# The products of a gated linear recurrence and of its gelu, from GpSimd to VectorE

## The chip, the cores and the metric

One core of a Trainium2 chip runs the whole program in one launch. The metric is the device time of one execution, in microseconds (us); the figure of a kernel is the median of its runs. Engines are named as in the profile: PE (TensorE; PEld its weight loads), DVE (VectorE), ACT (ScalarE), POOL (GpSimd), SP (SyncE, which issues most transfers).

## What is computed

Two transformer blocks over 512 tokens of width 1024, in float32. The change lies in the recurrent branch of the first block alone, 1024 channels wide:

```
gate = gelu(gr)
xc   = conv_b + sum over 4 taps of xpad[:, tap:tap+S] * conv_w[tap]
r    = sigmoid(xblk @ w_a + b_a);   i = sigmoid(xblk @ w_x + b_x)
log_a = -8 * r * softplus(-lru_lambda)
a    = exp(log_a);   b = sqrt(-expm1(2 * log_a)) * (i * xc)
h[t] = a[t] * h[t-1] + b[t]
rnn_out = h * gate
```

`xr` and `gr`, the inputs of the branch, are two of the projections of the first block. The gelu is the tanh form, so its argument is the polynomial `c * (g + 0.044715 g^3)` with `c = sqrt(2/pi)`.

## The kernel before

Activations lie transposed, channels on the 128 partitions and the 512 tokens along the free axis; a "tile" below is one 128x512 block of channels, and the recurrence has eight, tile 0 to tile 7. A float32 product on PE is made of three products of float32r parts: every operand is split into a high part (ACT, L271 `nc.scalar.copy`) and a low part (DVE, L272 `nc.vector.tensor_sub`). Weights arrive as "slabs" of 128x1024: SP loads `raw`, ACT casts `wh`, DVE subtracts `wl` (`slab`, L143), with 3 buffers for `raw` and 4 each for `wh` and `wl`. PE can begin a slab when its `wh` is there, and needs `wl` from the third matmul on.

`lru` (L930) is a generator that runs beside the value projection, the gates of the branch (`gates_T`) and later the first attention heads. `interleave` mixes the streams by a clock of PE's work; the framework's scheduler then fixes each engine's order, which is executed strictly in order. For tile m, `lru` does:

- `conv(m)`: DVE takes the projection `xr` out of PSUM (L937), POOL starts the convolution (L938), DVE adds three taps (L940), and the result `xc` is split into `xsh` and `xsl`.
- `gates(m - 1)`: two products of 3 matmuls each, then on ACT two tanh (L954, L955), a tanh `t2` (L956) and an exp (L957). Between the tables of tanh/exp and of the root ACT loads a table.
- `decay(m - 1)`: three DVE operations (L974 to L976), the root on ACT (L977), then root times d and times `xc` on POOL (L978, L979).
- `gelu(m)`: DVE takes `gr` out of PSUM (L962), ACT squares it (L963), POOL makes the polynomial in two operations (L964, L965), ACT applies tanh (L966).
- `scan(m - 1)`: DVE closes the gelu (L984), multiplies the input gate (L985), runs the scan (L987; ACT prepares its factor at L986), multiplies by the gate (L988), and the result is split into `rnh` (ACT) and `rnl` (DVE).

`rnn_pairs` (L1044) multiplies the eight `rnh`/`rnl` pairs by the next weights. ACT's `rnh` casts stand in one queue with its `wh` casts of the weight slabs.

```
nc.scalar.activation(q, g, AF.Square)
nc.gpsimd.tensor_scalar(q, q, 0.044715 * GELU_C, GELU_C, ALU.mult, ALU.add)
nc.gpsimd.tensor_mul(q, q, g)
```

Of the kernel before, what the change touches and what calls it, by code (L numbers as in the profile page):

```python
# [12 lines left out]
AF = mybir.ActivationFunctionType  # L13
ALU = mybir.AluOpType
# [6 lines left out]
GELU_C = math.sqrt(2.0 / math.pi)  # L21
# [73 lines left out]
class Net:  # L95
# [39 lines left out]
    def col(self, name, i=0, n=1):  # L135
        at, _ = COLS[name]
        return self.cols[:, at + i : at + i + n]
# [792 lines left out]
    def lru(self, act, rnn):  # L930
        nc = self.nc
        cw = lambda m, tap: self.col("conv_w", 4 * m + tap)
        st = {}

        def conv(m, ps):
            xr, xc = self.T("xr"), self.T("xc")
            nc.vector.tensor_mul(xr, ps, self.row)  # L937
            nc.gpsimd.tensor_scalar(xc, xr, cw(m, 3), self.col("conv_b", m), ALU.mult, ALU.add)  # L938
            for d in (1, 2, 3):
                nc.vector.scalar_tensor_tensor(  # L940
                    out=xc[:, d:], in0=xr[:, : S - d], scalar=cw(m, 3 - d), in1=xc[:, d:],
                    op0=ALU.mult, op1=ALU.add,
                )
            st[m] = dict(xc=xc, xs=self.split(xc, None, s="xs"))

        def gates(m):
            e = st[m]
            w = self.slab("w_rg", m, 256)
            pa, px = self.PS(), self.PS()
            self.mm3(pa, (w[0][:, 0:P], w[1][:, 0:P]), e["xs"], True, True)  # L950
            self.mm3(px, (w[0][:, P : 2 * P], w[1][:, P : 2 * P]), e["xs"], True, True)
            tr, ti, t2 = self.T("tr"), self.T("ti"), self.T("t2")
            col = lambda t: t[:, m : m + 1]
            nc.scalar.activation(tr, pa, AF.Tanh, bias=col(self.ba), scale=0.5)  # L954
            nc.scalar.activation(ti, px, AF.Tanh, bias=col(self.bx), scale=0.5)  # L955
            nc.scalar.activation(t2, tr, AF.Tanh, bias=col(self.sp2), scale=col(self.sp2))  # L956
            nc.scalar.activation(tr, tr, AF.Exp, bias=col(self.sp4b), scale=col(self.sp4))  # L957
            e.update(d=tr, ti=ti, t2=t2)

        def gelu(m, ps):  # L960
            g, q = self.T("gr"), self.T("gq")
            nc.vector.tensor_mul(g, ps, self.row)  # L962
            nc.scalar.activation(q, g, AF.Square)  # L963
            nc.gpsimd.tensor_scalar(q, q, 0.044715 * GELU_C, GELU_C, ALU.mult, ALU.add)  # L964
            nc.gpsimd.tensor_mul(q, q, g)  # L965
            nc.scalar.activation(q, q, AF.Tanh)  # L966
            st[m].update(g=g, q=q)

        def decay(m):

            e = st[m]
            d, t2 = e["d"], e["t2"]
            v = self.T("v")
            nc.vector.tensor_scalar_add(d, d, 0.5)  # L974
            nc.vector.scalar_tensor_tensor(out=v, in0=t2, scalar=1.0, in1=d, op0=ALU.add, op1=ALU.mult)
            nc.vector.scalar_tensor_tensor(out=d, in0=v, scalar=-2.0, in1=d, op0=ALU.add, op1=ALU.mult)  # L976
            nc.scalar.activation(t2, t2, AF.Sqrt)  # L977
            nc.gpsimd.tensor_mul(t2, t2, d)  # L978
            nc.gpsimd.tensor_mul(t2, t2, e["xc"])  # L979

        def scan(m):
            e = st.pop(m)
            d, t2, ti, g = e["d"], e["t2"], e["ti"], e["g"]
            nc.vector.scalar_tensor_tensor(out=g, in0=e["q"], scalar=1.0, in1=g, op0=ALU.add, op1=ALU.mult)  # L984
            nc.vector.scalar_tensor_tensor(out=ti, in0=ti, scalar=1.0, in1=t2, op0=ALU.add, op1=ALU.mult)  # L985
            nc.scalar.activation(d, d, AF.Copy, scale=-2.0, bias=-1.0)  # L986
            nc.vector.tensor_tensor_scan(t2, d, ti, 0.0, ALU.mult, ALU.add)  # L987
            nc.vector.scalar_tensor_tensor(out=t2, in0=t2, scalar=-0.5, in1=g, op0=ALU.mult, op1=ALU.mult)  # L988
            rnn.append(self.split(t2, None, s="rn"))

        for m in range(9):
            if m < 8:
                ps = yield from self.proj_T("w_xr", m, act)
                conv(m, ps)
            if m == 8:
                self.lru_tail = True
                yield 0.0
                yield self.lag(0.0, self.o["lg"])
            if m > 0:
                gates(m - 1)  # L1000
                yield 6.0
            if m < 8:
                gen = self.proj_T("w_gr", m, act)
                for _ in range(2):
                    yield next(gen)
                if m > 0:
                    decay(m - 1)
                ps = yield from gen
                gelu(m, ps)
            else:  # L1010
                yield 12.0
                decay(m - 1)
                yield 12.0
            if m > 0:
                scan(m - 1)
# [795 lines left out]
```

## Time and profile before

| what | value |
|---|---|
| median of 3 runs | 1905.67 us (1904.08 to 1912.12) |
| the profiled execution | 1912.68 us |
| its span, first to last instruction | 1910.9 us |
| busy share of the span | PE 98%, DVE 72%, ACT 45%, POOL 13% |
| mean granted TensorE clock | 0.988 of full speed |
| the recurrence, tile 0 to tile 7 | about 65 to 257 us of the span |

Times of day ("at 154.4") are us from the start of the span. A granted clock of 1.00 is 2.4 GHz, 0.50 is 1.2 GHz. In a timeline a row is one instruction or a run of equal ones, with the idle time of the engine just before it, and what ended that, in brackets. Durations of neighbouring rows on one engine overlap slightly.

### The profile page before, as it was taken

How to read it: one execution, taken by the hardware profiler on the slowest of the kernel's cores; microseconds unless marked ns; L12 is line 12 of the kernel's file. 1: busy time of each engine (PE TensorE's matmuls, PEld its weight loads, DVE VectorE, ACT ScalarE, POOL GpSimd, SP SyncE). 2: the span in 40 equal slices, each digit the busy share in tenths (PEclk: the TensorE clock that was granted, in tenths of full speed). 3: DMA queues.
4: the chain of work that ended last, by engine and by line, in shares of the span. 5: the costliest groups of instructions: out<-in, count | busy, mean ns of one | idle time of the engine just before them, and what ended most of it. 6: DMA issues, size and time to landing. Idle time of an engine off the chain costs nothing.

```text
span 1910.9 us, 26868 instructions
## 1 busy us (share of the span) xinstructions
PE 1866.7 (98%) x10392; PEld 1605.4 (84%) x10392; DVE 1366.8 (72%) x2582; ACT 868.5 (45%) x1499; POOL 239.1 (13%) x250
## 2 busy tenths in 40 slices
PE   8999999999989999999999999999999999999997
PEld 7887767888879999998887788888888899989896
DVE  7577787686788787776667856446556799887874
ACT  5456655454354334334334444233434555444443
POOL 3223310200300000002012110132300000000002
PEclk9999999999999999999999999999999999999998
DMA  5222322221453333334322122232432333322221
GB/s 188 79 93 83 105 67 78 89 77 45 142 172 95 99 110 100 95 103 144 98 78 67 67 83 73 99 122 90 153 129 93 122 110 133 110 89 100 100 85 60
DMA packets 57967, 192.23 MB, mean 101 GB/s; under 512 B 7040, under 2 KB 10144, under 8 KB 57840
## 3 DMA queue, kind: packets, MB, share of 16 engines
q1 hardware_dynamic: 50016, 170.78, 27.3%
q0 software_dynamic: 4832, 15.02, 2.6%
q10 hardware_dynamic: 2992, 4.72, 0.7%
q8 instruction: 81, 1.33, 0.3%
q14 instruction: 46, 0.38, 0.1%
HBM read 182.06 MB, written 8.43 MB: 100 GB/s over the span
## 4 chain that ended last, share of the span: by engine, by line
PE 80%; DVE 10%; ACT 4%; DMA 3%; issue 2%; POOL 1%; DVEq 0%; ACTq 0%; POOLq 0%; SPq 0%
PE ps L160 57%; PE u L160 10%; PE v L160 4%; PE p L160 2%; PE s L160 2%; PE o L160 2%; DVE wl L272 2%; PE pv L160 1%; PE pt L164 1%; DMA raw<-in_w_fd 1%; DMA raw<-in_w_fg 1%; ACT wh L271 1%; PE ps L164 1%; DMA raw<-in_w_down 1%; DMA raw<-in_w_fu 0%
## 5 line engine op out<-in xcount | busy, mean ns | idle before, releaser
L160 PE MATMUL ps<-xx,wh 128*128 128x512 f32 x1424 | 448.4, 396 | 2.7 <-ACT wh L271 2.7
L271 ACT CAST wh<-raw 128x1024 fp32r<-128x1024 f32 (+4 forms) x252 | 255.4, 1017 | 340.0 <-PE ps L160 195.6
L272 DVE TENSOR_TENSOR wl<-raw,wh 128x1024 fp32r<-128x1024 f32 (+4 forms) x252 | 313.1, 1243 | 84.1 <-ACT wh L271 82.3
L160 PEld LDWEIGHTS ps<-xx,wh 128*128 128x128 f32 x1424 | 263.8, 189 | 59.5 <-ACT wh L271 3.1
L160 PE MATMUL ps<-xx,wl 128*128 128x512 f32 x712 | 279.7, 393 | 1.6 <-DVE wl L272 1.6
L160 PE MATMUL ps<-wh,xx 128*128 128x512 f32 (+1 forms) x512 | 157.2, 380 | 5.7 <-ACT wh L271 5.7
L160 PEld LDWEIGHTS ps<-xx,wl 128*128 128x128 f32 x712 | 134.6, 189 | 31.7 <-DVE wl L272 2.5
L160 PEld LDWEIGHTS ps<-wh,xx 128*128 128x128 f32 x512 | 95.7, 192 | 22.2 <-ACT wh L271 5.7
L160 PE MATMUL ps<-ul,wh 128*128 128x512 f32 x256 | 100.1, 391 | 0.0
L160 PE MATMUL ps<-uh,wh 128*128 128x512 f32 x256 | 99.9, 391 | 0.0
L160 PE MATMUL ps<-uh,wl 128*128 128x512 f32 x256 | 99.6, 389 | 0.0
L160 PE MATMUL ps<-wl,xx 128*128 128x512 f32 (+1 forms) x256 | 96.7, 378 | 0.0
L480 POOL TENSOR_TENSOR sq<-sq,sq 128x512 f32<-128x512 f32 (+1 forms) x34 | 41.4, 1218 | 310.4 <-ACT sq L477 310.2
L375 ACT CAST sah<-sa 128x1024 fp32r<-128x1024 f32 x38 | 40.0, 1052 | 83.4 <-DVE sa L373 76.0
L160 PE MATMUL ps<-fah,wh 128*128 128x512 f32 (+1 forms) x200 | 73.6, 369 | 1.5 <-ACT fah L274 1.5
L160 PE MATMUL ps<-fal,wh 128*128 128x512 f32 (+1 forms) x200 | 73.4, 367 | 0.1
L160 PE MATMUL ps<-fah,wl 128*128 128x512 f32 (+1 forms) x200 | 72.8, 364 | 0.0
L1079 DVE TENSOR_TENSOR x<-ps,x 128x512 f32<-128x512 f32 x64 | 44.0, 688 | 39.0 <-PE ps L160 38.8
L160 PE MATMUL v<-f2h,wl 128*128 128x256 f32 x304 | 60.9, 283 | 0.0
L160 PEld LDWEIGHTS ps<-uh,wl 128*128 128x128 f32 x256 | 48.1, 188 | 10.3
L160 PEld LDWEIGHTS ps<-wl,xx 128*128 128x128 f32 x256 | 49.2, 192 | 8.3 <-DVE wl L272 0.4
L160 PEld LDWEIGHTS ps<-uh,wh 128*128 128x128 f32 x256 | 48.2, 188 | 9.2 <-ACT uh L271 0.3
(453 smaller groups left out, 4949.9 us busy)
## 6 DMA issues: line engine op xcount, KB each, us to landing
raw<-in_w_up SPq DMA_DIRECT2D x32, 512.0 KB, 3.5
raw<-in_w_down SPq DMA_DIRECT2D x32, 512.0 KB, 3.6
raw<-in_w_gate SPq DMA_DIRECT2D x24, 512.0 KB, 3.4
raw<-in_w_qkv SPq DMA_DIRECT2D x23, 512.0 KB, 3.6
raw<-in_w_fg SPq DMA_DIRECT2D x22, 512.0 KB, 3.4
raw<-in_w_fu SPq DMA_DIRECT2D x22, 512.0 KB, 3.5
raw<-in_w_fd SPq DMA_DIRECT2D x16, 512.0 KB, 3.4
raw<-in_w_conv SPq DMA_DIRECT2D x12, 512.0 KB, 3.5
```

What stands on the lines that cost most here:

```text
L160: self.nc.tensor.matmul(out, **k)
L164: self.nc.tensor.transpose(out, a, ident)
L271: nc.scalar.copy(hi, src)
L272: nc.vector.tensor_sub(lo, src, hi.bitcast(F32))
L375: nc.scalar.copy(ha, sa)
L480: eng.tensor_add(sq[0][:, sl], sq[0][:, sl], sq[1][:, sl])
L1079: nc.vector.tensor_add(self.x[m], ps, self.x[m])
```

## The change

The two products of the root, and the gelu's polynomial, move from POOL to DVE. The polynomial becomes one operation: the square is scaled on ACT in the operation that was there before, and one `scalar_tensor_tensor` adds the constant and multiplies by `g`. POOL keeps L938 alone of the recurrence. Per tile three DVE operations come and four POOL operations go.

```
         def gelu(m, ps):
             g, q = self.T("gr"), self.T("gq")
             nc.vector.tensor_mul(g, ps, self.row)
-            nc.scalar.activation(q, g, AF.Square)
-            nc.gpsimd.tensor_scalar(q, q, 0.044715 * GELU_C, GELU_C, ALU.mult, ALU.add)
-            nc.gpsimd.tensor_mul(q, q, g)
+            nc.scalar.activation(q, g, AF.Square, scale=math.sqrt(0.044715 * GELU_C))
+            nc.vector.scalar_tensor_tensor(out=q, in0=q, scalar=GELU_C, in1=g, op0=ALU.add, op1=ALU.mult)
             nc.scalar.activation(q, q, AF.Tanh)
...
             nc.scalar.activation(t2, t2, AF.Sqrt)
-            nc.gpsimd.tensor_mul(t2, t2, d)
-            nc.gpsimd.tensor_mul(t2, t2, e["xc"])
+            nc.vector.tensor_mul(t2, t2, d)
+            nc.vector.tensor_mul(t2, t2, e["xc"])
```

In the changed kernel one line is gone, so that later lines are numbered one lower: the polynomial is L964, the root L976, its products L977 and L978, the input gate L984, the scan L986, the multiplication by the gate L987. The scheduler also orders other instructions anew, between the second tile and the first pair of attention heads; elsewhere the order of every engine is as before. Numbers in names count buffers, and differ between the kernels.

ACT's queue at the end of tile 2 before, from the root to the split of the scan's result (`rnh`); `wh_1356` is the next slab that PE needs.

```order
L977 ACT_TABLE_LOAD
L977 ACTIVATE t_1171<-t_1171 128x512
L963 ACTIVATE gq_1249<-gr_1248 128x512
L986 ACTIVATE tr_1169<-tr_1169 128x512
L966 ACT_TABLE_LOAD
L966 ACTIVATE gq_1249<-gq_1249 128x512
L271 CAST rnh_1260<-t_1171 128x512
L271 CAST wh_1356<-raw_1355 128x1024
L1023 ACTIVATE gt_1295<-gt_1295 128x512
```

The same place with the change, where that slab is `wh_1352`.

```order
L976 ACT_TABLE_LOAD
L976 ACTIVATE t_1168<-t_1168 128x512
L963 ACTIVATE gq_1246<-gr_1245 128x512
L985 ACTIVATE tr_1166<-tr_1166 128x512
L965 ACT_TABLE_LOAD
L965 ACTIVATE gq_1246<-gq_1246 128x512
L271 CAST wh_1352<-raw_1351 128x1024
L271 CAST rnh_1256<-t_1168 128x512
L271 CAST wh_1399<-raw_1398 128x1024
```

The slab's cast stands ahead of the cast of the scan's result; at tile 1 the same swap is made, at the other tiles not.

DVE's queue at tile 6 before, from the operand d to the end of the scan.

```order
L976 SCALAR_TENSOR_TENSOR tr_1850<-v_1876,tr_1850 128x512
L272 TENSOR_TENSOR wl_2092<-raw_2090,wh_2091 128x1024
L985 SCALAR_TENSOR_TENSOR ti_1851<-ti_1851,t_1852 128x512
L987 SCALAR_TENSOR_TENSOR t_1852<-tr_1850,ti_1851 128x512
L988 SCALAR_TENSOR_TENSOR t_1852<-t_1852,gr_1769 128x512
```

The same with the change.

```order
L975 SCALAR_TENSOR_TENSOR tr_1843<-v_1869,tr_1843 128x512
L272 TENSOR_TENSOR wl_2084<-raw_2082,wh_2083 128x1024
L977 TENSOR_TENSOR t_1845<-t_1845,tr_1843 128x512
L964 SCALAR_TENSOR_TENSOR gq_1889<-gq_1889,gr_1888 128x512
L978 TENSOR_TENSOR t_1845<-t_1845,xc_1660 128x512
L984 SCALAR_TENSOR_TENSOR ti_1844<-ti_1844,t_1845 128x512
L986 SCALAR_TENSOR_TENSOR t_1845<-tr_1843,ti_1844 128x512
L987 SCALAR_TENSOR_TENSOR t_1845<-t_1845,gr_1763 128x512
```

The two products and the polynomial stand between the slab's low part and the input gate. On PE, four more transposes of the first attention heads (L164, `ps<-ident,z`) stand ahead of the first matmul on tile 6's `rnh`: ten in place of six.

## Rows read from the trace of the kernel before

**Rows 1.** Windows by stretch: us, busy (x instructions) of each engine, PEclk, DMA share, GB/s

```profile
64.00:256.00 192.00, 181.23 (x778) 148.06 (x777) 131.00 (x167) 109.17 (x151) 55.51 (x46) 0.96 0.28 87
96.00:128.00 32.00, 32.00 (x143) 26.50 (x142) 22.01 (x30) 19.27 (x30) 11.14 (x9) 1.00 0.31 99
...
130.00:140.00 10.00, 9.15 (x40) 7.22 (x39) 8.50 (x12) 4.87 (x7) 1.67 (x1) 1.00 0.23 71
...
151.50:154.40 2.90, 0.24 (x2) 0.01 (x1) 2.79 (x5) 1.56 (x2) 0.00 (x0) 1.00 0.00 0
154.40:155.90 1.50, 0.72 (x2) 0.28 (x2) 1.50 (x3) 1.15 (x2) 0.00 (x0) 0.76 0.00 0
155.90:161.60 5.70, 5.70 (x13) 4.46 (x14) 4.95 (x6) 2.30 (x4) 1.67 (x1) 0.50 0.38 115
...
242.50:247.20 4.70, 4.70 (x16) 3.91 (x17) 2.49 (x4) 4.02 (x7) 0.87 (x2) 0.50 0.04 11
...
256.30:300.00 43.70, 42.88 (x231) 33.81 (x231) 33.74 (x100) 23.90 (x56) 0.00 (x0) 1.00 0.27 85
```

**Rows 2.** Waits of PE from 60 to 270 us: us in total, times, longest

```profile
PE ps L160 <- ACT rnh L271: 5.5, 1, 5.5
PE ps L160 <- ACT wh L271: 2.7, 1, 2.7
PE ps L160 <- DVE wl L272: 1.6, 2, 0.9
PE ps L160 <- ACT xsh L271: 0.8, 1, 0.8
```

**Rows 3.** Timeline of ACT at the end of tile 2

```profile
144.53 0.63 ACT L977 ACTIVATE t<-t 128x512 f32<-128x512 f32 x1
...
147.48 1.28 ACT L966 ACT_TABLE_LOAD   x1
...
152.77 0.62 ACT L271 CAST rnh<-t 128x512 fp32r<-128x512 f32 x1 [1.97 <-DVE t L988]
153.30 1.04 ACT L271 CAST wh<-raw 128x1024 fp32r<-128x1024 f32 x1
```

**Rows 4.** Timeline of DVE at tile 2

```profile
144.63 0.68 DVE L976 SCALAR_TENSOR_TENSOR tr<-v,tr 128x512 f32<-128x512 f32 x1
...
148.92 1.77 DVE L985 SCALAR_TENSOR_TENSOR ti<-ti,t 128x512 f32<-128x512 f32 x1 [3.27 <-POOL t L979]
150.79 1.23 DVE L987 TENSOR_TENSOR_SCAN t<-tr,ti 128x512 f32<-128x512 f32 x1
152.05 0.69 DVE L988 SCALAR_TENSOR_TENSOR t<-t,gr 128x512 f32<-128x512 f32 x1
```

**Rows 5.** Groups by line and shape, 60 to 260 us: busy us, mean ns, idle before

```profile
L978 POOL TENSOR_TENSOR t<-t,tr 128x512 f32<-128x512 f32 x8 | 11.6, 1452 | 74.5 <-ACT t L977 48.6 <-DVE tr L976 26.0
L979 POOL TENSOR_TENSOR t<-t,xc 128x512 f32<-128x512 f32 x8 | 11.2, 1401 | 0.6
...
L985 DVE SCALAR_TENSOR_TENSOR ti<-ti,t 128x512 f32<-128x512 f32 x8 | 9.8, 1224 | 17.5 <-POOL t L979 17.5
...
L272 DVE TENSOR_TENSOR rnl<-t,rnh 128x512 fp32r<-128x512 f32 x8 | 5.9, 731 | 1.8 <-ACT rnh L271 1.4
...
L975 DVE SCALAR_TENSOR_TENSOR v<-t,tr 128x512 f32<-128x512 f32 x8 | 5.5, 689 | 0.2
L974 DVE TENSOR_SCALAR tr<-tr 128x512 f32<-128x512 f32 x8 | 3.4, 426 | 9.0 <-ACT tr L957 9.0
```

**Rows 6.** Timelines of DVE and PE around tile 6

```profile
221.58 0.68 DVE L937 TENSOR_TENSOR xr<-ps,row 128x512 f32<-128x512 f32 x1
...
233.56 1.22 DVE L272 TENSOR_TENSOR wl<-raw,wh 128x1024 fp32r<-128x1024 f32 x1
...
241.10 0.69 DVE L988 SCALAR_TENSOR_TENSOR t<-t,gr 128x512 f32<-128x512 f32 x1
...
236.21 0.82 PE L164 MATMUL ps<-ident,z 128*128 128x128 f32 x6
```

## The prediction

> **What bounds the kernel now.** I read the windows first, since a share over the whole span says nothing of one stage. PE is the bound: in an undisturbed stretch of the recurrence it never stops, 143 matmuls in 32 us at full clock, so one costs 0.224 us [rows 1]. From 64 to 256 us it was busy 181 of 192 us at a mean clock of 0.96, so this stage has holes; DVE was busy 131 us there and POOL 55.5. Behind the stage, from 256 to 300 us, PE idled 0.8 of 43.7 us: what is won in the stage should arrive at the end.
>
> The waits of PE name the holes [rows 2]: 5.5 us for an `rnh`, 2.7 for a `wh`, 1.6 for a `wl` in two waits, 0.8 for an `xsh`. Two are followed by a second loss. After PE had stood from 151.5 to 154.4 and again between 154.4 and 155.9, it ran until 161.6 at a granted clock of 0.50, which is 1.2 GHz in place of 2.4. After the 5.5 us, from its last transpose before `rnh` at 237.0 [rows 6] to 242.5, it did so for another 4.7 us [rows 1]. The wait of 0.9 us for a `wl` lies between 130 and 140 us, where the clock stayed at 1.00 [rows 1].
>
> So each hole has a price:
>
> - A, end of tile 2. From 151.5 to 161.6, 10.1 us, PE began 15 matmuls (2 and 13) after the last of the work before; they need 15 x 0.224 = 3.4. Lost: 6.7.
> - B, tile 6. 5.5 of standing, and half of the 4.7 us at half clock, 2.3. Lost: 7.8.
> - C and D. The `wl` wait that is not inside A, 0.9, and the `xsh` wait, 0.8. Lost: 1.7.
>
> Together 16.2 us, the most that the change can give, as it touches nothing outside this stage.
>
> **What ends these waits.** A is ended by the cast of a weight slab, but that cast was not slow: ACT stood 1.97 us for L988, cast `rnh`, and only then took the slab [rows 3]. L988 was late because DVE had stood 3.27 us for POOL's second product, and then needed 1.77 us for L985 where POOL was at work [rows 4]; L975, of the same form, takes 0.689 [rows 5]. B is the same chain at tile 6 with `rnh` itself wanted by PE. All eight tiles show DVE waiting for POOL, 17.5 us in all [rows 5].
>
> **The change, part by part.** Removed from the chain: POOL's two products, 1.45 and 1.40 us each tile, with POOL's polynomial between or behind them, and the lengthening of L985, 1224 against 689 ns [rows 5]. Added to DVE: 24 operations of 128x512 with two SBUF operands. The trace of before has no such product of f32 on DVE; the nearest rows are 426 ns (one tensor in) and 731 ns (`rnl`, some of them lengthened by POOL), and L975 at 689 is the same in everything but the arithmetic. I take 0.69: 24 x 0.69 = 16.6 us, in a stage where DVE has 192 - 131 = 61 us idle; its waiting for POOL alone was 17.5. I cost them at nothing as DVE work, and count them in the chain. The scaled square is the ACT operation that was there before. No transfer moves except two loads of bias strips on POOL's queue behind tile 6, which start earlier, and nobody waits for them. The end of the cover would be a DVE without idle time: see the fourth case.
>
> *A, replayed with these durations.* At tile 2 the third step L976 ends at 145.31, the root at 145.16 [rows 3, 4]. On DVE follow in the new order the first product to 146.0, polynomial to 146.7, second product to 147.4, input gate to 148.1, scan (1.23) to 149.3, multiplication by the gate to 150.0, against 152.74 before: 2.7 us earlier. More counts that ACT's slab cast now stands ahead of `rnh`. ACT prepares the scan's factor behind the first product (0.63, to 146.7), loads its table (1.28, to 147.9), applies tanh (0.63 like the root, to 148.6), casts the slab (1.04, to 149.6) [rows 3]. PE wants it at 151.5. `wl` follows on DVE behind the gelu's closing step: 150.0 + 0.69 + 1.22 = 151.9, and PE wants it with its third matmul, 0.45 us behind 151.5. Hole A closes within tenths: I count 6.5 of 6.7. With the products at 0.73 each step is later by 0.04 and nothing changes. C is the same pattern one tile earlier, with the same swap: 0.9.
>
> *B, replayed.* At tile 6 `wl` ends at 234.78 [rows 6]. Then product, polynomial, product, input gate (4 x 0.69) to 237.5, scan to 238.8, L988's counterpart to 239.5, against 241.79: 2.3 us earlier. At tile 5 the chain shortens too, so that DVE takes the last `xr` earlier than at 221.58; it did not wait for PE there [rows 6]. I take 1 us of that, between nothing and 1.5. Four transposes that now stand ahead fill 4 x 0.82 / 6 = 0.5 us. But D goes with the earlier `xr` (0.8), so PE arrives 0.8 sooner. The hole is 5.5 - 2.3 - 1 - 0.5 + 0.8 = 2.5 us. Whether the clock still falls behind it, no row decides: it fell behind the 2.7 us of A, and not behind 0.9. 2.5 is nearer to the former, so I let the 2.3 us at half clock stand. B gives 3.0, and D 0.8.
>
> Since A's end brings PE forward by 6.5 us but the chain by 2.7, the chain must gain the rest on tiles 3 to 5, or be late at tile 6. It should: it sheds 1 to 2 us on each, by the same count. That is the weakest link, and the second case prices it.
>
> *Sum.* 6.5 + 0.9 + 3.0 + 0.8 = 11.2 us. What is late next is tile 7's `rnh`, which PE met without a wait before, and the first attention heads, whose DVE order was made anew. I take 0 for both, between 1 us won and 3 lost, from the 0.8 us that PE idled behind the stage and the 2.5 of a hole like B's remainder.
>
> The profiled execution took 1912.68 us and would take 1901.5. It lies 7.0 above the median of 1905.67, and the three runs spread over 8; against the median the forecast is **1894.5 us**.
>
> **The rivals.**
>
> 1. *As worked out*: A gone, B reduced. 1894.5, between 1889.5 (the whole 16.2) and 1896.
> 2. *B stays whole.* A goes, 6.5, with C; but tiles 3 to 5 do not make up for PE's lead, so the `xr` and the root of tile 6 come no sooner against PE and 0 to 2 of B and D is won. For it: DVE did not wait for PE at the last `xr` [rows 6], so the chain ran by itself there. Against: it sheds POOL's 2.85 us each tile for 1.4. Gain 6.5 + 0.9 + 1 = 8.4 less up to 3 in the heads: 1897 to 1900.
> 3. *Nothing to win*: something else ends the waits just behind POOL, as ACT's table loads of 1.28 us or a buffer of the slabs. Then 0 to 3 us, 1903 to 1906. Against: the cast of `rnh` waited for DVE, and the slab's cast stood behind it alone [rows 3]. That the change does not do what it says is excluded by the order: the four operations are off POOL.
> 4. *Slower: DVE becomes what PE waits for.* In DVE's queue the first product stands waiting for the root, and at tile 5 a `wl` of the next slab stands behind both. If DVE's 131 us and 16.6 more, with new waits, fill the stage, PE waits for `wl` on each tile. It decides when these waits reach 192 - 147.6 = 44 us. Up to 16.6 us, 1922; half of it, 1914, as the lengthened rows come back. Against: at tile 2 the root was done before L976, so the first product waits for nothing. The Trainium skill, in "Perfetto Trace Analysis", section "Optimizing Scalar/DVE Operations", says that work may be worth moving off VectorE, even to GpSimd, where VectorE is saturated; that speaks against the change on this branch alone, and by it the time would be this case's. The trace does not bear the condition out, with VectorE at 131 of 192 us, and the same section doubts that moving work between these two helps at all.
>
> **How the numbers follow.** About 0.5% (9.5 us) is what a measurement of this kernel tells from no change. Case 1: 0.60; its gain of 11.2 lies above that bound by less than the heads could take, which the second case carries. Case 2: 0.26. Case 3: 0.07. Case 4: 0.07. Case 1 counts as faster, 2 and 3 as the same but for 0.02 of case 2 that reach past the bound: 0.62 faster, 0.31 the same, 0.07 slower. The range takes case 1 down to the whole 16.2 and a us or two of the runs' own spread, 1888, and up through case 2 into case 3, 1903. What is left out is case 4 and the end of case 3.
>
> **What would show it.** In the profile after: PE's waits for `wh` at about 150 us and for `wl` at about 133 gone, and full clock from 150 to 160; DVE's 17.5 us of waiting for POOL at the input gate gone, and that operation at 0.69; the products near 0.69 us; PE's wait for tile 6's `rnh` at 2 to 3 us in place of 5.5; POOL's busy time down. Wrong it would be if the products take well over 0.75, if PE waits anew for `wl` or `xsh` in tiles 3 to 6, or if the stage ends 11 us earlier and the heads give it back.

## The result, and the profile after

The changed kernel took 1890.59 us (median of 4 runs, 1887.68 to 1895.34); the kernel before took 1908.29 beside it (4 runs). The ratio is 0.9909, with a 95% interval of 0.9892 to 0.9925: faster by 0.9%, some 17 us, which is more than the 0.5% that a measurement can tell. The profiled execution took 1895.34 us with a span of 1893.6, against 1912.68 and 1910.9.

The first view is PE's waits from 60 to 256 us in the kernel after (columns: us in total, times, longest). It answers to [rows 2].

```profile
PE ps L160 <- ACT rnh L271: 1.6, 1, 1.6
PE ps L160 <- DVE gt L1033: 0.3, 1, 0.3
```

The waits for `wh`, `wl` and `xsh` are gone, and the one for tile 6's `rnh` is 1.6 us in place of 5.5. The windows of the same kernel answer to [rows 1]: length, busy time of PE, PEld, DVE, ACT and POOL, then PE's granted clock, the DMA share and GB/s.

```profile
64.00:256.00 192.00, 190.12 (x865) 155.78 (x864) 151.50 (x237) 120.17 (x175) 13.80 (x14) 1.00 0.32 98
150.00:160.00 10.00, 10.00 (x46) 8.27 (x45) 6.75 (x10) 5.86 (x9) 1.67 (x1) 1.00 0.37 112
224.00:256.00 32.00, 30.12 (x159) 23.30 (x158) 28.26 (x66) 21.39 (x40) 0.00 (x0) 1.00 0.27 81
```

PE was busy 190.12 us of the 192 in place of 181.23, and at full clock throughout. DVE has 151.50 us of work there in place of 131.00, POOL 13.80 in place of 55.51. The groups of instructions from 60 to 250 us (busy us, mean ns of one, idle before and its releaser) answer to [rows 5].

```profile
L977 DVE TENSOR_TENSOR t<-t,tr 128x512 f32<-128x512 f32 x8 | 5.5, 687 | 0.5 <-ACT t L976 0.2
L978 DVE TENSOR_TENSOR t<-t,xc 128x512 f32<-128x512 f32 x8 | 5.5, 687 | 0.1
L964 DVE SCALAR_TENSOR_TENSOR gq<-gq,gr 128x512 f32<-128x512 f32 x8 | 5.5, 686 | 0.5 <-ACT gq L963 0.4
L984 DVE SCALAR_TENSOR_TENSOR ti<-ti,t 128x512 f32<-128x512 f32 x8 | 5.5, 688 | 0.2
L940 DVE SCALAR_TENSOR_TENSOR xc<-xr,cols,xc 128x511 f32<-128x511 f32 x8 | 6.0, 750 | 4.7 <-POOL xc L938 4.7
```

The products and the polynomial take 0.69 us each, DVE's 17.5 us of waiting at the input gate are gone, and that operation (L984, before L985) fell from 1224 to 688 ns. The timelines of DVE and PE at tile 6 answer to [rows 6].

```profile
210.76 0.68 DVE L937 TENSOR_TENSOR xr<-ps,row 128x512 f32<-128x512 f32 x1
...
222.74 1.22 DVE L272 TENSOR_TENSOR wl<-raw,wh 128x1024 fp32r<-128x1024 f32 x1
...
227.85 0.69 DVE L987 SCALAR_TENSOR_TENSOR t<-t,gr 128x512 f32<-128x512 f32 x1
...
226.41 1.25 PE L164 MATMUL ps<-ident,z 128*128 128x128 f32 x10
229.24 0.73 PE L160 MATMUL ps<-rnh,wh 128*128 128x512 f32 x2 [1.58 <-ACT rnh L271]
```

To see whether the gain was kept, I follow the score matmuls of the attention heads (`s`), which come behind the recurrence. This is the tile view of `s` in the kernel before: after the count stand the shortest, median and longest ns, and the start of the first and the last.

```profile
L160 PE MATMUL s<-qkh,qkh x64: 221/398/497, 256.3 to 444.3; 64*128 64x128 f32 x16, 64*128 64x256 f32 x16, 64*128 64x384 f32 x16, 64*128 64x512 f32 x16
```

And in the kernel after:

```profile
L160 PE MATMUL s<-qkh,qkh x64: 221/399/497, 240.4 to 427.6; 64*128 64x128 f32 x16, 64*128 64x256 f32 x16, 64*128 64x384 f32 x16, 64*128 64x512 f32 x16
```

The first `s` starts 15.9 us earlier and the last 16.7; the spans differ by 17.3. All of it was won in the recurrence and the first heads, and kept.

For a single execution a measure is wanted that leaves out what lies around the stage, as the traces begin up to 1.4 us apart, and executions differ behind the stage too. Two matmuls can be told in every trace: the first product of the gates (`xsh`), and the one `s` in the heads that PE begins after a wait for ACT's `zq`. Before and after (PE's timelines):

```profile
83.74 0.39 PE L160 MATMUL ps<-xsh,wh 128*128 128x512 f32 x1
329.27 0.49 PE L160 MATMUL s<-qkh,qkh 64*128 64x512 f32 x1 [0.42 <-ACT zq L762]
...
83.60 0.39 PE L160 MATMUL ps<-xsh,wh 128*128 128x512 f32 x1
312.72 0.49 PE L160 MATMUL s<-qkh,qkh 64*128 64x512 f32 x1 [0.43 <-ACT zq L762]
```

Between the two it is 245.5 us before and 229.1 after. Below, "lead" is by how much this stretch is shorter than the 245.5 of before: 16.4 us for the changed kernel, and 16.4 again in its second profile. The expectations go by the last `s`, which is blurred: from the `s` behind `zq` to the last one it takes 114.9 to 115.1 us in five of the thirteen traces and 113.4 to 113.7 in the others, whatever the kernel. In the five PE ran at half clock for a time between 362 and 392 us, in the others not; it is worth some 1.6 us. These are the windows of two runs that differ by one useless product at tile 6 (told of below, with three and with four products):

```profile
362.00:392.00 30.00, 29.09 (x148) 22.24 (x147) 23.58 (x87) 18.18 (x52) 0.00 (x0) 0.94 0.17 55
...
362.00:392.00 30.00, 29.09 (x159) 22.54 (x158) 25.03 (x89) 19.61 (x55) 0.00 (x0) 1.00 0.19 57
```

### The profile page after: what moved, and what is told of

Read it like the earlier page. It is cut to its first block, busy times and chain, and to the rows that moved or that the text cites. A ratio compares the mean times of both kernels' runs of the same rounds, so it can differ in the third digit from the quotient of the medians.

```text
span 1893.6 us, 26855 instructions
## 1 busy us (share of the span) xinstructions
PE 1859.6 (98%) x10392; PEld 1601.2 (85%) x10392; DVE 1373.4 (73%) x2606; ACT 868.0 (46%) x1499; POOL 197.7 (10%) x218
## 4 chain that ended last, share of the span: by engine, by line
PE 84%; DVE 8%; ACT 3%; issue 2%; DMA 2%; POOL 0%; DVEq 0%; ACTq 0%; POOLq 0%; SPq 0%
PE ps L160 60%; PE u L160 10%; PE v L160 5%; PE p L160 2%; PE s L160 2%; PE o L160 2%; DVE wl L272 1%; PE pv L160 1%; PE pt L164 1%; DMA raw<-in_w_down 1%; ACT L L846 1%; DMA raw<-in_w_fu 0%; PE ps L164 0%; ACT wh L271 0%; DMA raw<-in_w_fg 0%
```

## The experiments

**One half at a time.** The first two kernels make one half of the change. The products alone:

```
-            nc.gpsimd.tensor_mul(t2, t2, d)
-            nc.gpsimd.tensor_mul(t2, t2, e["xc"])
+            nc.vector.tensor_mul(t2, t2, d)
+            nc.vector.tensor_mul(t2, t2, e["xc"])
```

> The two root products on VectorE, the polynomial left on GpSimd as two operations. ACT's order at tiles 1 and 2 is that of the kernel before: the slab's cast stands behind the split of the scan's result. Theory (the chain's length decides): the chain of tile 2 ends 3 us earlier by the products alone, the slab is cast at 151 of the old clock, so hole A is under 1 us without a stretch at half clock, hole B 1 to 2 us; gain 14 to 17 us, nearly the whole. Rival (the new order of ACT's queue decides): A stays at 2 us or more with its half clock; gain 6 to 10 us.

Measured: 1896.81 us, ratio 0.9945 (0.9926 to 0.9964), lead 9.2. The polynomial alone:

```
-            nc.scalar.activation(q, g, AF.Square)
-            nc.gpsimd.tensor_scalar(q, q, 0.044715 * GELU_C, GELU_C, ALU.mult, ALU.add)
-            nc.gpsimd.tensor_mul(q, q, g)
+            nc.scalar.activation(q, g, AF.Square, scale=math.sqrt(0.044715 * GELU_C))
+            nc.vector.scalar_tensor_tensor(out=q, in0=q, scalar=GELU_C, in1=g, op0=ALU.add, op1=ALU.mult)
```

> The polynomial alone on VectorE as one operation, the two root products left on GpSimd. Theory: the chain of each tile loses only the polynomial that stood between the two products (0.7 us) and the lengthening of the input gate (0.5 to 1.1 us), so A shrinks by 1 to 2 us and B by 1 to 2; VectorE still waits over 10 us for GpSimd's second product; gain 2 to 8 us. Rival (GpSimd's shared work as such is the harm, whichever part goes): about half of the 17 us, 8 to 9.

Measured: 1899.58 us, ratio 0.9951 (0.9933 to 0.9969), lead 8.9. Neither expectation came out whole: the products were to win 14 to 17 us with hole B at 1 to 2, and the polynomial was to shrink A by 1 to 2 only. Each half by itself closes hole A: PE keeps a wait of 0.8 us with the products and 0.4 with the polynomial, for a `wl`, and the clock from 150 to 160 us is 1.00 in both. At tile 2 of both kernels ACT still casts `rnh` (at 148.18 and 146.89) ahead of the slab (148.71 and 147.42), so the swap of these two casts was not needed. Hole B stays large in each. PE's timeline, products alone:

```profile
233.22 1.22 PE L160 MATMUL ps<-rnh,wh 128*128 128x512 f32 x2 [3.98 <-ACT rnh L271]
```

And the polynomial alone:

```profile
231.31 1.22 PE L160 MATMUL ps<-rnh,wh 128*128 128x512 f32 x2 [4.64 <-ACT rnh L271]
```

The clock falls behind both: from 224 to 256 us it was 0.89 and 0.95, against 1.00 with the whole change. With the polynomial alone the input gate still waits for POOL's second product on each tile, 12.8 us in all, and the polynomial beside POOL's first product is lengthened from 0.69 to 1.78 us (DVE's timeline at tile 6):

```profile
224.92 1.78 DVE L964 SCALAR_TENSOR_TENSOR gq<-gq,gr 128x512 f32<-128x512 f32 x1
...
227.86 0.69 DVE L984 SCALAR_TENSOR_TENSOR ti<-ti,t 128x512 f32<-128x512 f32 x1 [1.16 <-POOL t L978]
```

With the products alone, the timeline of DVE and POOL at tile 6 shows why:

```profile
226.57 0.93 POOL L964 TENSOR_SCALAR gq<-gq 128x512 f32<-128x512 f32 x1 [11.09 <-ACT gq L963]
226.94 1.10 DVE L978 TENSOR_TENSOR t<-t,tr 128x512 f32<-128x512 f32 x1
227.59 1.60 POOL L965 TENSOR_TENSOR gq<-gq,gr 128x512 f32<-128x512 f32 x1
228.07 1.66 DVE L979 TENSOR_TENSOR t<-t,xc 128x512 f32<-128x512 f32 x1
```

Each product on DVE takes 1.10 and 1.66 us where it takes 0.69 alone, and each ends 0.54 us behind the end of POOL's operation beside it (227.50 and 229.19). The Trainium skill, in "SBUF — State Buffer", section "SBUF: two separate sides", says that a VectorE operation with two inputs in SBUF and a GpSimd operation that reads SBUF exclude one another, and that whichever comes second is blocked until the first is done. The trace agrees: the time behind POOL's end is the same in both rows, whatever the time before it. It is so throughout: in the traces of the kernel before, of the two halves and of the next run, 45 float32 operations of 128x512 on DVE with both operands in SBUF (the scan left aside) began while one of POOL's products or operations of the polynomial ran, and every one ended 0.54 or 0.55 us behind it. The eight that read one operand from PSUM and began beside such an operation took 0.68 or 0.69 us all the same. POOL is held up in its turn: in the traces before and after, its first step of the convolution (L938) took 0.77 us alone, and 1.60 to 1.84 us where DVE had begun the low part of a 128x1024 slab before it, or at most 0.11 us behind it; that low part took its usual 1.22.

**POOL's hindrance by itself.** The changed kernel, with four products on POOL at each tile that feed nothing:

```
             nc.vector.scalar_tensor_tensor(out=v, in0=t2, scalar=1.0, in1=d, op0=ALU.add, op1=ALU.mult)
             nc.vector.scalar_tensor_tensor(out=d, in0=v, scalar=-2.0, in1=d, op0=ALU.add, op1=ALU.mult)
             nc.scalar.activation(t2, t2, AF.Sqrt)
+            for _ in range(4):
+                nc.gpsimd.tensor_mul(self.T("junk"), v, v)
```

> The changed kernel with four products of v by itself on GpSimd in each tile, written to tiles that nobody reads, so that GpSimd works beside the new VectorE chain as it did before, and nobody waits for it. Theory (the hand-over and GpSimd's own slowness were the harm): 0 to 4 us slower than the changed kernel. Rival (GpSimd and VectorE hinder each other, and that was most of it): the VectorE operations beside it lengthen from 0.69 to 1.2 us and more, the wait for tile 6's result grows to 3 us or more with a stretch at half clock, 5 us and more slower than the changed kernel.

Measured: 1911.61 us, ratio 1.002 (1.0002 to 1.0038); the lead is -4.8, 21.2 us less than after the change (the last `s` at 447.2, 19.6 later). The whole gain is gone. The groups from 60 to 250 us:

```profile
L978 POOL TENSOR_TENSOR junk<-v 128x512 f32<-128x512 f32 x28 | 42.5, 1545 | 60.3 <-DVE v L974 60.3
L980 DVE TENSOR_TENSOR t<-t,xc 128x512 f32<-128x512 f32 x7 | 9.7, 1390 | 0.1
L964 DVE SCALAR_TENSOR_TENSOR gq<-gq,gr 128x512 f32<-128x512 f32 x8 | 9.7, 1210 | 0.4 <-ACT gq L963 0.4
L979 DVE TENSOR_TENSOR t<-t,tr 128x512 f32<-128x512 f32 x7 | 7.7, 1098 | 0.2 <-ACT t L976 0.2
```

Nobody waits for these products: DVE's only wait for POOL is the 4.7 us for `xc` that it has after the change too. But they lengthen the three moved operations from 0.69 to 1.39, 1.21 and 1.10 us: 7 x 0.70 + 8 x 0.52 + 7 x 0.41 = 12.0 us. The third step, the input gate and the low parts of the slabs lose another 6 us in the same way (0.69 to 0.93 and 0.85, 1.22 to 1.31, 0.42 to 0.52). The theory that only the hand-over and POOL's slowness were the harm falls.

**VectorE's idle time.** As many useless products on DVE, which test the fourth case of the rivals:

```
             rnn.append(self.split(t2, None, s="rn"))
+            for _ in range(4):
+                nc.vector.tensor_mul(self.T("junk"), t2, t2)
```

> The changed kernel, with four products of 128x512 into tiles that nobody reads on VectorE behind each tile's scan and split, 32 x 0.69 = 22 us in all; VectorE would be busy 173 of the stage's 192 us. They need no other engine. It tests the fourth case of the rivals and stands beside the run with 42.5 us of products on GpSimd. Theory (VectorE's time is spare only off the chain; these stand ahead of the next tile's xr and put it off by 2.8 us, and tiles catch up in part): PE waits again for rnh, xsh or wl, 5 to 15 us in the stage. Case 4 as the prediction counted it (it decides only when waits fill 44 us): nothing or up to 2 us. Rival (VectorE fills at once): 16 us and more, the slower side of the kernel before.

Measured: 1907.94 us, ratio 1.0009 (0.9994 to 1.0025); the lead is -1.0, 17.4 us less than after the change (the last `s` at 442.7, 15.1 later). PE's waits from 60 to 256 us, then the group of the added products from 60 to 250:

```profile
PE ps L160 <- ACT xsh L271: 6.3, 1, 6.3
PE ps L160 <- ACT rnh L271: 4.2, 1, 4.2
PE ps L160 <- DVE wl L272: 0.9, 1, 0.9
...
L990 DVE TENSOR_TENSOR junk<-t 128x512 f32<-128x512 f32 x28 | 17.4, 684 | 0.0
```

DVE had 40 us idle in the stage after the change; with 28 of the added operations in it DVE was busy 156 of the 192 us, and none of its other operations took longer. The chain of the tiles was late all the same. Case 4 as counted (up to 2 us) falls. The loss lies above what I expected (5 to 15) and is as large as the rival had it (16 and more), but not for the rival's reason: VectorE was not full.

**The part of `rnh`.** The kernel before, with the high part made on DVE, so that ACT's queue does not hold a slab's cast behind it:

```
-            rnn.append(self.split(t2, None, s="rn"))
+            hi, lo = self.R("rnh"), self.R("rnl")
+            nc.vector.tensor_copy(hi, t2)
+            nc.vector.tensor_sub(lo, t2, hi.bitcast(F32))
+            rnn.append((hi, lo))
```

> The kernel before, with the high part of the scan's result made on VectorE and no longer on ACT, so that ACT's slab cast waits for no scan. Theory A (PE waits at tile 2 because of ACT's queue alone): hole A closes with its half clock, 5 to 7 us faster than before. Theory B (the slab's low part stands behind the same chain in VectorE's queue, so the chain's length must shrink): PE's wait for the high part turns into one of 3 us for the low part; within 2 us of the kernel before.

Measured: 1909.87 us, ratio 1.0008 (0.9988 to 1.0028), lead -1.1. PE's waits from 60 to 256 us:

```profile
PE ps L160 <- DVE rnh L990: 4.2, 1, 4.2
PE ps L160 <- DVE wl L272: 4.1, 2, 3.7
PE ps L160 <- ACT xsh L271: 2.2, 1, 2.2
```

The wait for `wh` became one of 3.7 us for the `wl` of the same slab, which stands behind the same chain on DVE. Moving the cast alone wins nothing; the chain has to be shorter.

**The size of hole B, and the clock.** In the changed kernel, tile 6's chain alone is made longer by two, three, four and seven products on DVE. The edit, with N for that number:

```
             nc.vector.tensor_mul(t2, t2, e["xc"])
+            if m == 6:
+                for _ in range(N):
+                    nc.vector.tensor_mul(self.T("junk"), v, v)
```

> The changed kernel, with two products of v by v into a tile that nobody reads on VectorE at tile 6 alone, between the root's third step and its scan: the chain of hole B is 2 x 0.69 = 1.4 us longer, at no other place. In the changed kernel PE waits 1.6 us there and the clock stays at 1.00. In the new order four more transposes of 0.125 us stand ahead of PE's wait. Theory (a hole of this size costs itself and no clock, as after the change): the wait is 1.6 + 1.4 - 0.5 = 2.5 us, the clock stays at 1.00 and the stage ends 1 us later. Rival (the prediction's own step, by which the clock falls behind a hole of 2.5 us as it did behind the 2.7 of hole A): the wait is about 2.5, and behind it 3 to 5 us run at half clock, the stage ends 3 to 4 us later. Second rival (the wait is not set by this chain): it stays at 1.6 or below.

> As the run with two products more at tile 6, with three: VectorE's order and PE's are the same but for the one product. There PE stood 1.88 us for rnh and the clock stayed at 1.00. Each product costs 0.60 us start to start, so the wait should be 2.5 us, which is the very hole that the prediction left standing with its half clock. The prediction's step: behind it 3 to 5 us at half clock, and the last score matmul 3 us later than with two. Rival: the clock stays at 1.00, and the stage ends 0.6 us later.

> The same with four products: a wait of 3.1 us. The prediction's step: half clock behind it for 3 to 5 us. Rival (the clock falls with this hole, not with the one before): 1.00 at three products and below it here. Second rival: 1.00 in both.

> The same with seven products, a wait of 4.9 us, close to the 5.5 of hole B before the change. All theories: the clock falls to half for 4 to 5 us behind it; it says that the place does not matter for the clock, and gives the price of such a hole in the new order: the last score matmul 3.0 us later for the standing and 2 more for the clock than with two products, 432.8 us in place of 427.8. If the clock stays at 1.00 here too, it was something else than the hole that lowered it before the change.

PE's wait and the window of 230 to 240 us with two products:

```profile
230.03 0.73 PE L160 MATMUL ps<-rnh,wh 128*128 128x512 f32 x2 [1.88 <-ACT rnh L271]
...
230.00:240.00 10.00, 9.96 (x42) 7.91 (x43) 7.90 (x13) 7.21 (x11) 0.00 (x0) 1.00 0.01 2
```

And with three:

```profile
230.28 0.79 PE L160 MATMUL ps<-rnh,wh 128*128 128x512 f32 x2 [2.48 <-ACT rnh L271]
...
230.00:240.00 10.00, 9.72 (x35) 7.58 (x36) 7.91 (x13) 7.46 (x12) 0.00 (x0) 0.83 0.01 2
232.00:234.00 2.00, 2.00 (x6) 1.57 (x5) 1.25 (x3) 2.00 (x5) 0.00 (x0) 0.50 0.00 0
```

| products added at tile 6 | PE's wait for `rnh` | clock, 230 to 240 us | lead | last `s` |
|---|---|---|---|---|
| none | 1.58 | 1.00 | 16.4 | 427.6 |
| two | 1.88 | 1.00 | 14.5 | 427.8 |
| three | 2.48 | 0.83 | 12.5 | 431.1 |
| four | 3.10 | 0.83 | 11.6 | 431.0 |
| seven | 1.84 (for `gr`) and 3.10 | 0.66 | 9.2 | 432.9 |

With two, the wait grew by 0.3 and not by 0.9: the order was made anew, which put the polynomial behind the scan, so that from the last `xr` to PE's matmul on `rnh` it is 0.94 us longer, and sixteen transposes in place of ten, 0.66 us more, stand ahead of PE's wait. The clock stayed, so this run did not test the step. Its lead fell by 1.9 even so, as PE also waited 1.0 us for a `wl` and 1.0 for the heads' `s` later on, in place of 0.3 for `gt`.

The order is the same with three, and there the step is tested. The third product lengthened the wait by 0.6, as expected, and the lead fell by 2.0: 0.6 for the standing, and 1.4 for the stretch at 1.2 GHz. The last `s` came 3.3 us later and so suggests more, but 1.6 of that is the half clock between 362 and 392 us, which the run with three had and the run with two had not, and the two traces begin 0.4 apart. So the prediction was right that a hole of 2.5 us at this place costs the clock too, and it cost 1.4 where the prediction had 2.3. With four the lead fell by another 1.0, of which 0.6 is the longer wait; the last `s` did not move, since this run had full clock from 362 to 392. With seven PE stood twice, 4.9 us in all as expected, and the lead is 5.3 below that with two: 3.1 of standing and some 2 of clock, as expected. Each of these four is one execution, of 1886.04, 1894.18, 1895.44 and 1902.84 us.

**The last operation on POOL.** The changed kernel, with the convolution's first step on DVE too:

```
-            nc.gpsimd.tensor_scalar(xc, xr, cw(m, 3), self.col("conv_b", m), ALU.mult, ALU.add)
+            nc.vector.tensor_scalar(xc, xr, cw(m, 3), self.col("conv_b", m), ALU.mult, ALU.add)
```

> The changed kernel with the first step of the convolution (L938, one tensor_scalar of 128x512 for each tile) on VectorE as well, so that GpSimd computes nothing in the stage; 8 x 0.43 = 3.4 us more on VectorE, by L974, and its waits of 4.7 us for GpSimd go. Theory (what is left in the stage is PE's wait of 1.6 us and tenths): 0 to 2 us faster than the changed kernel, within what can be measured; PE's wait for rnh at tile 6 at 0.5 to 1.6. Rival (the eight operations still lengthen VectorE's and hold the chain on each tile): 3 us and more. Other side (the order made anew puts a slab's low part late): 1 to 3 us slower.

Beside it on the same chip, the changed kernel again:

> The changed kernel itself, beside the others on one chip. Expected: 1888 to 1894 us, ratio to the kernel before 0.991; in the stage the same waits of PE, 1.6 us for rnh and 0.3 for gt, and the last score matmul at about 427.6 us. The time between that and the first residual add is expected to differ from the earlier profile by up to 9 us, as it did between earlier runs.

Measured: 1893.48 us, ratio to before 0.9932 (0.9912 to 0.9952), with the convolution on DVE; 1888.46, 0.9916 (0.9894 to 0.9939), without. The intervals overlap, so the times do not tell the two apart; the lead is 15.1 with the convolution on DVE and 16.4 without, 1.3 us lost in the stage. (The last `s` starts at 427.6 and 427.8; the run without had the half clock between 362 and 392 us.) PE's waits with the convolution on DVE:

```profile
PE ps L160 <- ACT rnh L271: 1.4, 1, 1.4
PE ps L160 <- DVE wl L272: 1.0, 1, 1.0
```

So the 4.7 us that DVE waits for POOL in the changed kernel won nothing when they went, and what came is the "other side" of the expectation: the order made anew puts a slab's low part late, a wait of 1.0 us for `wl` that the changed kernel does not have. No run had a larger lead than the changed kernel.

## Why the prediction was right, and where its terms were off

The forecast was 1894.5 us, and 1890.59 was measured; the holes closed by the mechanism that the prediction names. The gain is further off than these two times: the sum had 11.2 us, and the lead is 16.4 (17.7 between the medians). Part of the nearness is luck, since the forecast was taken from a median of 1905.67, and the kernel before came to 1908.29 with a fourth run.

The sum can be checked hole by hole, by the starts of the same matmul in both traces. The last matmul of the projection behind the last `xr` starts here in PE's timeline before:

```profile
218.05 0.39 PE L160 MATMUL ps<-xx,wl 128*128 128x512 f32 x1
```

and after:

```profile
209.85 0.39 PE L160 MATMUL ps<-xx,wl 128*128 128x512 f32 x1
```

PE is 8.2 us earlier there, 0.1 of which is the start of the traces; 9.8 at the transposes ahead of the wait for `rnh` (236.21 [rows 6] and 226.41), 15.9 at the first `s`, and 16.5 at the `s` behind `zq`.

- **A and C** came, 8.1 us together in place of 6.5 + 0.9: no wait of PE and full clock from 128 to 160 us. One argument in it falls: the swap of ACT's casts, which "counts more" there, is absent in the kernels with one half, and A closed there as well. That the chain was shorter was enough.
- **D** came at 1.6 in place of 0.8. PE's idle time shows only 1.0 of it, with the 0.2 us for `xsl` that stood behind the wait for `xsh`; this hole cost 0.6 beyond the idle time by which the prediction priced it.
- **The cost of the added work** came as worked out: 0.69 us each, from L975. The prediction counted POOL's lengthening of DVE in one operation alone, L985. It holds for whatever DVE does with two operands in SBUF beside POOL's products and polynomial. The two halves show what that is worth: leads of 9.2 and 8.9, neither near zero nor adding up to the 16.4 of both. Each alone closes A, and each leaves B large, at 4.0 and 4.6 us of standing with half clock behind it, since DVE is still hindered by POOL at tile 6 or waits for it. How much of the whole gain is the end of the hand-over to POOL, and how much the end of its hindrance, no run separates.
- **B was the mis-sized term.** The prediction had 5.5 - 2.3 - 1 - 0.5 + 0.8 = 2.5 us of standing left, with the half clock behind it: a gain of 3.0. Measured is 1.58 at full clock, a gain of 3.9 + 2.3 = 6.2, and 6.1 by the starts (15.9 less 9.8). The chain behind `wl` shortened as worked out: from the start of `wl` to PE's matmul on `rnh` it was 242.5 - 233.56 = 8.9 us [rows 2, 6] and is 229.24 - 222.74 = 6.5, so 2.4 against 2.3. What was off is "I take 1 us of that, between nothing and 1.5", for the last `xr`. DVE took `xr` 3.5 us later than the matmul at 218.05 before (221.58) and 0.9 us later than the same one after (210.76): 2.6 us won in place of 1, outside the bounds that I gave. The chain had gained on tiles 3 to 5 more than PE's lead took back. PE for its part arrived 1.2 us sooner, counted from that matmul, against 0.3 in the prediction: 1.6 for D less 0.4 for the transposes. So 5.5 - 2.4 - 2.6 + 1.2 = 1.7, and 1.6 was measured.
- **The half clock** went with the smaller hole. That it stands behind 2.5 us and not behind 1.9 is what the runs at tile 6 show, with 2.48 and 1.88. So 0.9 us of error in the chain made 3.2 us of error in the sum.
- **The weakest link**, whether tiles 3 to 5 make up for PE's lead, held; with it falls the second case, in which B stays whole.
- **Tile 7 and the first heads**, taken at 0 between 1 us won and 3 lost, gave 0.6. With 8.1 + 1.6 + 6.1 that makes the 16.4. Their order was made anew; no run separated that.
- **"The most that the change can give"**, 16.2 us, was reached although PE still stands 1.58 us at tile 6: it has 6.7 + 0.9 for A and C and 0.8 for D, and these were worth 8.1 and 1.6.
- **The fourth case** did not come, but its deciding point was wrong. It had DVE as the bound only once its waits fill 44 us; 17.4 us of added work ahead of the next tiles, with DVE still idle for 36 of the 192 us, already cost the whole gain.

## What to carry to other kernels

An engine's idle share tells nothing of a chain that runs through it: count what the chain sheds and what is added to it, from tile to tile up to the hole that it ends in. Where VectorE and GpSimd work at the same time on operands in SBUF, price VectorE's as longer, also where nobody waits for GpSimd's result. What a part of such a move is worth depends on the hole that it still leaves: here each half alone closed hole A, and only both together brought hole B down to where the clock stayed. And price a hole of PE both without and with the clock behind it: here the clock stayed behind 1.88 us of standing, and 2.48 us cost 1.4 beyond themselves.

## What was not expected of the hardware

Useless work on GpSimd, 42.5 us of it, cost PE 21.2 us of lead without any engine waiting for it; useless work of 17.4 us on VectorE cost 17.4.

Executions of one kernel differ where the change does not touch them: in the half clock between 362 and 392 us told of above, and further on. In the first profile of the changed kernel PE stood 2.53 us for an `f1h`, and part of the next 10 us ran at half clock (PE's timeline, then the windows):

```profile
547.31 0.61 PE L160 MATMUL v<-f1h,sah 128*128 128x256 f32 x2 [2.53 <-ACT f1h L271]
...
540.00:550.00 10.00, 6.73 (x46) 6.04 (x46) 8.04 (x14) 3.40 (x7) 0.00 (x0) 0.88 0.53 175
550.00:560.00 10.00, 10.00 (x55) 10.00 (x56) 5.45 (x23) 5.26 (x9) 1.07 (x2) 0.61 0.32 107
```

In the second profile of the same kernel that wait is absent (the same two windows):

```profile
540.00:550.00 10.00, 7.95 (x55) 7.45 (x55) 7.37 (x23) 6.17 (x11) 1.07 (x2) 0.88 0.59 197
550.00:560.00 10.00, 10.00 (x80) 9.92 (x80) 7.60 (x17) 4.31 (x8) 1.06 (x2) 0.95 0.11 35
```

The last `s` starts at 427.6 and 427.8 in the two, and the first residual addition at 581.1 and 573.9: 7 us apart, and so are the spans, 1893.6 and 1886.9. The profile of the kernel before has the wait too, with 2.7 us. What decides either was not looked into; the runs of the changed kernel lie about as far apart, 1887.68 to 1895.34 us.
